# Buffers of the S5 output stage: two for the coefficients of C, the staging ring for the Toeplitz tile, results in halves

## The chip, the cores and the metric

One core of one Trainium2 chip. The metric is the device time of one execution in microseconds (us); less is better. The core has TensorE (PE; its weight loads are shown as PEld), VectorE (DVE), ScalarE (ACT), GpSimd (POOL) and SyncE (SP), which here only issues DMAs. DMAs are issued from the queues of SP and ScalarE, and 16 DMA engines carry them.

## The reference, cut to what matters

One step of a two-layer encoder over 2,192 tokens (16 meta, 2,048 of the prompt, 8 x 16 of running streams). Layer 0 is an S5 diagonal complex state-space model beside an xLSTM mLSTM; layer 1 is retention beside an RG-LRU. The change lies in the S5 part of layer 0:

```python
    _, _, h_re, h_im = lax.associative_scan(_cplx_combine, (a_re, a_im, bu_re, bu_im), axis=1)
    y = (jnp.einsum('btgp,gcp->btgc', h_re, c_re.astype(F32))
         - jnp.einsum('btgp,gcp->btgc', h_im, c_im.astype(F32)))
    y = y.reshape(bsz, T, W_A) + d.astype(F32) * uf
    y = jax.nn.gelu(y)
    y = y * jax.nn.sigmoid(y @ w_glu.astype(F32) + b_glu.astype(F32))
```

There are 32 groups of 16 channels and 64 complex states. All matrix products of the kernel that need it are made of three products of rounded halves (lines 121 to 125).

## The kernel before, in words

The kernel runs six phases; the change is in the second, `phase_l0` (line 354). This phase projects layer 0's input in three thirds of the tokens. In each third, `mtile` makes 16 tiles: 8 of the mLSTM's input (`isz` 0, with convolution and SiLU) and 8 of its gate (`isz` 1). A tile loads 512 KB of weights (line 379, on SP's queue, two buffers `wr1`), ScalarE rounds them to `wh` (line 382 by way of 105), GpSimd makes the rest `wl` (line 118), TensorE makes 48 products of 384 columns into one of four PSUM buffers (`pm1`), and ScalarE evicts them (lines 395 and 397). `values` (line 437) makes the mLSTM's values from pairs of finished tiles and needs no weights of line 379.

The normalised input of the next blocks of tokens is loaded again by `reload` (line 461): three loads per block (line 467) into the ring `ut1` of four buffers of 4 KB per partition, then `split` rounds them into `ub` (lines 105 and 109) as soon as the block that lies there has been read for the last time. There are twelve such loads.

Beside these tiles runs the generator `s5` (line 765); after each tile from the third on it is taken one step further (line 509). It has three parts:

- States (lines 772 to 859): eight steps, q = 0 to 7, of four groups each.
- Outputs (lines 861 to 936), pool `s5y`, again eight steps. For each q, `toeplitz` (line 884) loads the inputs `ur` (`s5u`, line 761), forms the coefficients `ca` (`s5ca`, lines 895 to 899) of C times the powers of the decay, multiplies them with B on TensorE (line 904), copies the result to `kp` (lines 907 and 908), writes it to HBM (line 909) and reads it back eight times, shifted, as the Toeplitz tile `tz` (`s5tz`, line 912). Then TensorE makes the outputs of two halves of 8 time steps (lines 927 to 931), ScalarE copies them to `yst` (line 934), and one DMA per half and q writes them to HBM (line 935). All tiles here have one buffer, but for the PSUM tag `s5p` with three.
- Gated unit (lines 941 to 1003), pool `s5g`: 32 loads bring the outputs back in another order (`s5gy`, line 950, on SP's queue), ScalarE takes the Gelu (line 961), and a product with `w_glu`, whose weights lie in the ring `ut1` (`p.room`, line 956), gates them. In the program this part comes in the last third (`p.loaded`, lines 485 and 938).

Program order is not the order of execution. The program is handed to a planner (`schedule_with_timeline_sim`, line 2168), which simulates it and fixes the order of the instructions on every engine and queue ahead of the run. Among instructions that are ready in its simulation the one that comes first in the program goes first; a tile takes a buffer of its tag when the first instruction that writes it is placed. On the chip each engine and queue then works strictly in that order, and an instruction that waits holds up all behind it. Pools that are closed hand their memory on tile by tile (`reuse_waits="tile"`), so the tiles of `s5g` wait for the last readers of those that lay there before.

Of the kernel before, what the change touches and what calls it, by code (L numbers as in the profile page):

```python
# [9 lines left out]
F32 = mybir.dt.float32  # L10
# [16 lines left out]
NCH = T // 16  # L27
# [10 lines left out]
def P(e, name, bufs=1, side=None):  # L38
    return e.tc.tile_pool(name=name, bufs=bufs, side=side, reuse_waits="tile")
# [6 lines left out]
def opn(e, name, bufs=1, side=None, psum=False):  # L46

    if psum:
        cm = e.tc.tile_pool(name=name, bufs=bufs, space=MemoryType.PSUM, side=side, reuse_waits="tile")
    else:  # L50
        cm = P(e, name, bufs, side)
    e.cms[name] = cm
    return cm.__enter__()
# [49 lines left out]
def split(nc, h, l, x, pool=False, act=True, fine=False):  # L103

    (nc.scalar.copy if act else nc.vector.tensor_copy)(h, x)  # L105
    if fine:
        narrow(nc, l, x, h, OP.subtract)
    else:
        (nc.gpsimd if pool else nc.vector).tensor_tensor(l, x, h, op=OP.subtract)  # L109
# [244 lines left out]
def phase_l0(e):  # L354

    nc, tc = e.nc, e.tc
# [3 lines left out]
    sb = opn(e, "b_sb", 2)  # L360
    xp = opn(e, "b_x", 2)
# [75 lines left out]
    def values(h, ut, tiles, parts):  # L437
# [8 lines left out]
        for c, nt, kind, row in tiles:  # L446
# [9 lines left out]
            nc.gpsimd.tensor_add(g, g, vo[:nt, 256:264].rearrange("p (a b) -> p a b", a=2))  # L456

    s5g = s5(e, ps)
    e.s5.loaded = False
    e.s5.room = lambda: xp.tile([128, 1024], F32R, name="ut1", bufs=4)  # L460
    def reload(bi):
        blk, b0, n = blks[bi]
        pool = e.ub_pool if bi % 3 < 2 else sb
        t = e.ub[bi] = pool.tile([128, 2, KD, 384], F32R, name=f"ub{bi % 3}", bufs=1)
        for c, nt, kind, row in blk:
            ur = xp.tile([128, KD, 128], F32, name="ut1", bufs=4)[:, :, :nt]
            nc.sync.dma_start(ur, e.u[:, :, c:c + nt])
            split(nc, t[:, 0, :, c - b0:c - b0 + nt], t[:, 1, :, c - b0:c - b0 + nt], ur)

    steps = 0  # L470
    for third in range(3):
# [6 lines left out]
        if third > 0:  # L478

            early = [mtile(third, 0, 0, ut, pg, parts),  # L480
                     mtile(third, third % 2 == 0, third % 2, ut, pg, parts)]
            for g in early:
                next(g)
            reload(2 * third + 1)
            e.s5.loaded = third == 2
# [82 lines left out]
def s5_base(e, ps):  # L568
# [4 lines left out]
    with P(e, "s5bs", side="right") as sb:  # L573
# [35 lines left out]
        v.tensor_scalar(csn, csn, -1.0, math.pi / 2, op0=OP.mult, op1=OP.add)  # L609
        nc.scalar.activation(csn, csn, AF.Sin)  # L610
        s5_phasors(v, sb, s5, csn, sn, mag, par)
        s5_turns(e, sb)

# [80 lines left out]


def s5_phasors(v, sb, s5, cs, sn, mag, par):


# [57 lines left out]
def s5_u(e, sb, q):  # L756

    ur = sb.tile([128, 2, 4, NCH], F32, name="s5u")
    gs = slice(4 * (q % 2), 4 * (q % 2) + 4)
    for hh in range(2):  # L760
        e.nc.sync.dma_start(ur[:, hh], e.ua[q // 2, 8 * hh:8 * hh + 8, :, gs, :].rearrange("s c g n -> (s c) g n"))
    return ur


def s5(e, ps):

    nc, v, tc = e.nc, e.nc.vector, e.tc
    p = e.s5
# [92 lines left out]
    with P(e, "s5y", side="right") as sb:  # L861

        pw, cc = p.pw, p.b
        for j, nm in enumerate(("re", "im")):
            cr = sb.tile([128, 4, 17, 16], F32, name="s5tm2").rearrange("p a b c -> p (a b c)")
            cr = cr[:, :512].rearrange("p (a b c) -> p a b c", a=4, b=2)
            for q in range(2):
                nc.sync.dma_start(cr[:, :, q, :], e.i["s5_c_" + nm].rearrange("a (m g) c p -> (g c) (a m) p", m=4))
            pc = ps.tile([128, 4, 128], F32, name="s5p", bufs=3)
            for m in range(4):  # L870
                nc.tensor.transpose(pc[:, m, :], cr[:, m].rearrange("p a b -> p (a b)"), e.ident)
            v.tensor_copy(cc[j].rearrange("p (m g) c -> p m (g c)", m=4), pc)


        d16 = sb.tile([128, 8], F32, name="s5d16")
        dd = sb.tile([128, 8, 16], F32, name="s5dd")
        v.memset(dd, 0.0)
        for j in range(4):
            js = slice(32 * j, 32 * j + 16)
            nc.sync.dma_start(d16[js], e.i["s5_d"].rearrange("a (q j c) -> j c (a q)", c=16, j=4)[j])  # L880
            v.tensor_tensor(dd[js], e.ident[js, None, js].to_broadcast([16, 8, 16]),
                            d16[js, :, None].to_broadcast([16, 8, 16]), op=OP.mult)

        def toeplitz(q):
            ur = s5_u(e, sb, q)
            gs = slice(4 * q, 4 * q + 4)
            cp = sb.tile([128, 2, 4, 17], F32, name="s5cp")
            v.tensor_copy(cp[UP, 0], pw[UP, 0, gs])
            v.tensor_scalar(cp[LO, 0], pw[LO, 1, gs], -1.0, None, op0=OP.mult)
            v.tensor_scalar(cp[UP, 1], pw[UP, 1, gs], -1.0, None, op0=OP.mult)  # L890
            v.tensor_scalar(cp[LO, 1], pw[LO, 0, gs], -1.0, None, op0=OP.mult)
            ca = sb.tile([128, 4, 17, 16], F32, name="s5ca")
            tmp = sb.tile([128, 4, 17, 16], F32, name="s5tm2")
            sh = [128, 4, 17, 16]
            v.tensor_tensor(ca, cp[:, 0, :, :, None].to_broadcast(sh), cc[0][:, gs, None, :].to_broadcast(sh),
                            op=OP.mult)
            v.tensor_tensor(tmp, cp[:, 1, :, :, None].to_broadcast(sh), cc[1][:, gs, None, :].to_broadcast(sh),
                            op=OP.mult)
            v.tensor_add(ca, ca, tmp)
            kp = sb.tile([128, 23, 16], F32, name="s5kp")  # L900
            v.memset(kp[:, 0:7, :], 0.0)
            pk = ps.tile([128, 256], F32, name="s5p", bufs=3)
            for j in range(4):
                nc.tensor.matmul(pk[32 * j:32 * j + 32], p.bb[:, 4 * q + j:4 * q + j + 2, :].rearrange("p a b -> p (a b)"),
                                 ca[:, j, 0:16, :].rearrange("p a b -> p (a b)"), start=True, stop=True,
                                 tile_position=(0, 32 * j), skip_group_check=True)
            nc.scalar.copy(kp[:, 7:23, :], pk.rearrange("p (a b) -> p a b", b=16))
            v.tensor_add(kp[:, 7, :], kp[:, 7, :], dd[:, q, :])
            nc.sync.dma_start(e.kp[q], kp)
            tz = sb.tile([128, 4, 16, 16], F32, name="s5tz")  # L910
            for k in range(8):
                nc.sync.dma_start(tz[16 * k:16 * (k + 1)],
                                  e.kp[q].rearrange("(g c) a b -> c g a b", g=4)[:16, :, 7 - k:23 - k, :])
            return ur, ca, tz

        for q in range(8):
            ur, ca, tz = toeplitz(q)
            for mh in range(2):
                yst = sb.tile([128, 4, NCH], F32, name="s5yst")
                for g0 in (0, 2):  # L920
                    py = ps.tile([128, 2, NCH], F32, name="s5p", bufs=3)
                    for j in range(2):
                        g = g0 + j
                        t0 = tz[:, g, 0:8, :].rearrange("p a b -> p (a b)")
                        t1 = tz[:, g, 8:16, :].rearrange("p a b -> p (a b)")
                        if mh == 0:
                            nc.tensor.matmul(py[:, j, :], t0, ur[:, 0, g, :], start=True, stop=False)
                        else:
                            nc.tensor.matmul(py[:, j, :], t1, ur[:, 0, g, :], start=True, stop=False)
                            nc.tensor.matmul(py[:, j, :], t0, ur[:, 1, g, :], start=False, stop=False)  # L930
                        nc.tensor.matmul(py[:, j, :],
                                         ca[:, g, 1 + 8 * mh:9 + 8 * mh, :].rearrange("p a b -> p (a b)"),
                                         ee[:, 4 * q + g, :], start=False, stop=True)
                    nc.scalar.copy(yst[:, g0:g0 + 2, :], py)
                nc.scalar.dma_start(e.ys[q // 2, mh, :, 4 * (q % 2):4 * (q % 2) + 4, :], yst)
            yield
    cls(e, "s5ee", "s5kb", "s5keep", "s5par")
    while not p.loaded:
# [2 lines left out]
    with P(e, "s5g", side="right") as sb:  # L941
# [47 lines left out]
        for b in range(8):  # L989
            view, n, gs = nxt  # L990
# [1108 lines left out]


PHASES = [phase_in0, phase_l0, phase_mlstm, phase_out0, phase_in1, phase_ret]


# [68 lines left out]
```

## Time and profile before

| | |
|---|---|
| Median of 3 runs (lowest, highest) | 3088.95 us (3086.74, 3089.72) |
| The profiled execution: time | 3077.24 us |
| The profiled execution: span from first to last instruction | 3075.5 us |
| Mean granted TensorE clock, as a share of full speed | 0.992 |
| Busy share of the span | TensorE 97%, VectorE 54%, ScalarE 34%, GpSimd 32% |

Times in the trace are microseconds from the start of the span. In a timeline row, the idle time of the engine ahead of the instruction stands in brackets with what ended it; a row with x3 merges three instructions in a row. "SPq" and "ACTq" are the DMA issues of SP and ScalarE.

### The profile page before, as it was taken

Reading aid. Unit: us, or ns where it says so; the run is one execution under the profiler, and the core shown is the slowest. Engines: PE = TensorE matmul, PEld = TensorE weight load, DVE = VectorE, ACT = ScalarE, POOL = GpSimd, SP = SyncE. Lnnn points to the kernel's source line nnn. Section 1 sums busy time; section 2 is a strip of 40 time slices with the busy share of each in tenths; the row PEclk is TensorE's granted clock in tenths of the full one; section 3 lists DMA queues with packets and bytes.
Section 4 is the critical chain, followed back from the end, with each engine's and each line's share of the span. In section 5 each row is a group of like instructions: output and inputs, shape, how many; then the busy total and the mean of one; then the engine's idle time right before and its main releaser. Section 6 shows DMA issues by size and latency. Waiting matters only on the chain.

```text
span 3075.5 us, 45329 instructions
## 1 busy us (share of the span) xinstructions
PE 2979.3 (97%) x17435; PEld 2696.1 (88%) x17435; DVE 1671.9 (54%) x3410; ACT 1059.5 (34%) x1860; POOL 982.1 (32%) x1160
## 2 busy tenths in 40 slices
PE   8999999998999989999999999999999999999999
PEld 7999989987988877777899999999998897888887
DVE  4845884454537772333446677767700036656563
ACT  4213443435254533211235555555511122121111
POOL 6305655445336751111111111111100024433431
PEclk9999999998999999999999999999999999999999
DMA  6447455556735557564441111111122167544442
GB/s 206 155 104 222 154 165 166 167 158 149 223 101 172 184 152 249 161 196 149 154 127 52 52 52 52 47 51 48 44 80 80 49 189 220 149 130 122 139 121 75
DMA packets 447298, 404.81 MB, mean 132 GB/s; under 512 B 43593, under 2 KB 392977, under 8 KB 447082
## 3 DMA queue, kind: packets, MB, share of 16 engines
q1 hardware_dynamic: 335340, 272.36, 31.2%
q10 hardware_dynamic: 111742, 129.56, 12.5%
q8 instruction: 137, 2.24, 0.3%
q14 instruction: 79, 0.65, 0.1%
HBM read 266.35 MB, written 135.49 MB: 131 GB/s over the span
## 4 chain that ended last, share of the span: by engine, by line
PE 61%; DVE 6%; DMA 4%; ACT 1%; issue 1%; POOL 1%; SPq 0%; DVEq 0%; POOLq 0%; ACTq 0%
PE p_pm L124 9%; PE p_pm L125 8%; PE p_pm L123 8%; PE r_pm L125 4%; PE r_pm L124 4%; PE r_pm L123 4%; PE pa L123 3%; PE pa L124 3%; PE pa L125 3%; PE pc L1388 1%; DVE p_d L1754 1%; PE pn L1385 1%; DVE p_xc L550 1%; PE r_o L1956 1%; DMA d_gb<-m_zb 1%
## 5 line engine op out<-in xcount | busy, mean ns | idle before, releaser
L123 PE MATMUL p_pm<-pu,p_wh 128*128 128x384 f32 (+1 forms) x1568 | 512.1, 327 | 0.2 <-ACT pu L105 0.2
L124 PE MATMUL p_pm<-pu,p_wh 128*128 128x384 f32 (+1 forms) x1568 | 511.8, 327 | 0.0
L125 PE MATMUL p_pm<-pu,p_wl 128*128 128x384 f32 (+1 forms) x1568 | 511.4, 326 | 0.0
L123 PE MATMUL pm<-ub,wh 128*128 128x384 f32 (+1 forms) x1136 | 377.2, 333 | 2.0 <-ACT vo L452 1.8
L124 PE MATMUL pm<-ub,wh 128*128 128x384 f32 (+1 forms) x1136 | 376.4, 331 | 1.6 <-DVE ub L109 1.6
L125 PE MATMUL pm<-ub,wl 128*128 128x384 f32 (+1 forms) x1136 | 372.9, 331 | 2.3 <-POOL wl L118 1.9
L123 PEld LDWEIGHTS p_pm<-pu,p_wh 128*128 128x128 f32 x1568 | 294.2, 188 | 1.8 <-issue 1.2
L124 PEld LDWEIGHTS p_pm<-pu,p_wh 128*128 128x128 f32 x1568 | 294.5, 188 | 1.0 <-issue 0.8
L125 PEld LDWEIGHTS p_pm<-pu,p_wl 128*128 128x128 f32 x1568 | 294.4, 188 | 0.0
L118 POOL TENSOR_TENSOR wl<-wr,wh 128x256 fp32r<-128x256 f32 x188 | 177.8, 976 | 203.7 <-ACT wh L105 203.7
L123 PEld LDWEIGHTS pm<-ub,wh 128*128 128x128 f32 x1136 | 214.4, 189 | 7.8 <-issue 4.0
L123 PE MATMUL r_pm<-roh,r_gh 128*128 128x512 f32 x544 | 218.8, 403 | 1.2 <-ACT roh L105 0.8
L125 PE MATMUL r_pm<-roh,r_gl 128*128 128x512 f32 x544 | 217.5, 401 | 1.5 <-DVE r_gl L109 1.5
L125 PEld LDWEIGHTS pm<-ub,wl 128*128 128x128 f32 x1136 | 214.4, 189 | 4.7 <-POOL wl L118 2.6
L124 PE MATMUL r_pm<-rol,r_gh 128*128 128x512 f32 x544 | 217.9, 401 | 0.4 <-DVE rol L109 0.4
L124 PEld LDWEIGHTS pm<-ub,wh 128*128 128x128 f32 x1136 | 214.7, 189 | 3.1 <-DVE ub L109 2.1
L109 POOL TENSOR_TENSOR p_wl<-p_wr,p_wh 128x1024 fp32r<-128x1024 f32 x34 | 81.8, 2406 | 385.2 <-ACT p_wh L105 385.2
L109 POOL TENSOR_TENSOR p_xcl<-p_xc,p_xch 128x384 fp32r<-128x384 f32 (+1 forms) x48 | 46.8, 976 | 245.5 <-ACT p_xch L105 209.0
L125 PEld LDWEIGHTS r_pm<-roh,r_gl 128*128 128x128 f32 x544 | 103.3, 190 | 24.0 <-DVE r_gl L109 2.4
L123 PEld LDWEIGHTS r_pm<-roh,r_gh 128*128 128x128 f32 x544 | 103.1, 190 | 22.7 <-ACT roh L105 1.3
L124 PEld LDWEIGHTS r_pm<-rol,r_gh 128*128 128x128 f32 x544 | 103.2, 190 | 21.0 <-DVE rol L109 0.7
L1754 DVE RECIPROCAL p_d<-p_d 128x384 f32<-128x384 f32 (+1 forms) x48 | 116.7, 2432 | 0.6
(731 smaller groups left out, 6751.0 us busy)
## 6 DMA issues: line engine op xcount, KB each, us to landing
wr<-in_ev_w_in_dram SPq DMA_DIRECT2D x47, 512.0 KB
p_wr<-in_od_w_in_dram SPq DMA_DIRECT2D x40, 512.0 KB
d_in<-p_o ACTq DMA_DIRECT2D x80, 192.0 KB
m_rw<-d_grow SPq DMA_DIRECT2D x18, 512.0 KB
s5u<-d_ua SPq DMA_DIRECT2D x32, 274.0 KB
d_v<-vo ACTq DMA_DIRECT2D x68, 128.0 KB
m_va<-d_v SPq DMA_DIRECT2D x17, 512.0 KB
d_h<-o_x ACTq DMA_DIRECT2D x17, 512.0 KB
```

Source lines behind the costliest of these rows:

```text
L109: (nc.gpsimd if pool else nc.vector).tensor_tensor(l, x, h, op=OP.subtract)
L118: nc.gpsimd.tensor_tensor(out[:, c], a[:, c], b[:, c], op=op)
L123: nc.tensor.matmul(out, a[0], b[0], start=start, stop=False, **kw)
L124: nc.tensor.matmul(out, a[0], b[1], start=False, stop=False, **kw)
L125: nc.tensor.matmul(out, a[1], b[0], start=False, stop=stop, **kw)
L550: v.tensor_scalar(out, x(3), pc[:, m, cw + 3:cw + 4], pc[:, m, cb:cb + 1], op0=OP.mult, op1=OP.add)
L1385: nc.tensor.matmul(pn[:n], c.qs[:, 2 * h + k, :n], ct[h][:, k, :], start=False, stop=k == 1)
L1388: nc.tensor.matmul(pc, c.kw[:n, h, 128 * k:128 * (k + 1)], c.va[:n, h, :], start=True, stop=True)
L1754: v.reciprocal(d[:, :n], d[:, :n])
L1956: nc.tensor.matmul(po, qk[:, h, :], S[:, h, :], start=False, stop=True)
```

## The change

`ca` gets two buffers. `tz` is no longer a tile of its own in pool `s5y`, but a tile of the ring `ut1`, whose four buffers serve the reloads and the weights of the gated unit as well. `yst` holds two of the four groups in place of all four, has two buffers, and is written to HBM after each copy: 32 writes of half the size in place of 16.

```diff
     e.s5.room = lambda: xp.tile([128, 1024], F32R, name="ut1", bufs=4)
+    e.s5.stage = lambda: xp.tile([128, 1024], F32, name="ut1", bufs=4)
...
-            ca = sb.tile([128, 4, 17, 16], F32, name="s5ca")
+            ca = sb.tile([128, 4, 17, 16], F32, name="s5ca", bufs=2)
...
-            tz = sb.tile([128, 4, 16, 16], F32, name="s5tz")
+            tz = p.stage().rearrange("p (g a b) -> p g a b", g=4, a=16)
...
             for mh in range(2):
-                yst = sb.tile([128, 4, NCH], F32, name="s5yst")
                 for g0 in (0, 2):
+                    yst = sb.tile([128, 2, NCH], F32, name="s5yst", bufs=2)
                     py = ps.tile([128, 2, NCH], F32, name="s5p", bufs=3)
...
-                    nc.scalar.copy(yst[:, g0:g0 + 2, :], py)
-                nc.scalar.dma_start(e.ys[q // 2, mh, :, 4 * (q % 2):4 * (q % 2) + 4, :], yst)
+                    nc.scalar.copy(yst, py)
+                    gs = slice(4 * (q % 2) + g0, 4 * (q % 2) + g0 + 2)
+                    nc.scalar.dma_start(e.ys[q // 2, mh, :, gs, :], yst)
```

## Rows read from the trace of the kernel before

**Rows 1.** The page, busy us (share of the span) and instructions of each engine.

```profile
PE 2979.3 (97%) x17435; PEld 2696.1 (88%) x17435; DVE 1671.9 (54%) x3410; ACT 1059.5 (34%) x1860; POOL 982.1 (32%) x1160
```

**Rows 2.** Busy time by stretch: stretch, length, engines, granted clock, DMA share, GB/s.

```profile
467.00:679.00 212.00, 207.33 (x1404) 198.21 (x1403) 111.08 (x160) 76.35 (x142) 99.21 (x134) 0.99 0.53 162
640.00:664.00 24.00, 20.54 (x150) 18.17 (x149) 15.91 (x34) 9.91 (x20) 10.75 (x20) 0.93 0.63 197
...
702.00:709.30 7.30, 4.32 (x26) 3.69 (x24) 3.98 (x10) 3.42 (x4) 4.01 (x8) 1.00 1.23 144
709.30:726.50 17.20, 7.00 (x33) 5.75 (x34) 4.20 (x9) 12.23 (x16) 4.79 (x9) 0.50 1.05 213
```

**Rows 3.** Timeline of TensorE, 640 to 724 us: start, length, instruction, idle before.

```profile
643.44 0.51 PE L427 MATMUL pg<-xc,gw 128*8 128x192 f32 x8 [2.49 <-ACT xc L421]
...
713.34 0.59 PE L123 MATMUL pm<-wvh,xbh 128*128 128x264 f32 x1 [5.64 <-ACT xb L397]
...
722.32 0.59 PE L123 MATMUL pm<-wvh,xbh 128*128 128x264 f32 x1 [5.03 <-ACT xb L397]
```

**Rows 4.** Timeline of ScalarE, 664 to 740 us.

```profile
697.25 1.05 ACT L105 CAST wh<-wr 128x1024 fp32r<-128x1024 f32 x1
...
710.89 2.03 ACT L961 ACTIVATE s5gy<-s5gy 128x2192 f32<-128x2192 f32 x1 [4.43 <-DMA s5gy<-d_ys]
...
718.58 1.28 ACT L961 ACT_TABLE_LOAD   x1 [2.49 <-DMA s5gy<-d_ys]
...
724.59 1.06 ACT L105 CAST wh<-wr 128x1024 fp32r<-128x1024 f32 x1
```

**Rows 5.** Timeline of SP's queue, 664 to 740 us.

```profile
671.41 0.40 SPq L379 DMA_DIRECT2D wr<-in_ev_w_in_dram  x1
679.06 31.84 SPq L950 DMA_DIRECT2D s5gy<-d_ys  x32
...
714.49 1.87 SPq L379 DMA_DIRECT2D wr<-in_ev_w_in_dram  x2
```

**Rows 6.** Timelines of TensorE, SP and VectorE, 526 to 551 us: one round.

```profile
526.85 0.40 PE L931 MATMUL s5p<-s5ee,s5ca 128*128 128x137 f32 x2
527.05 0.82 SPq L761 DMA_DIRECT2D s5u<-d_ua  x2
527.53 1.72 DVE L895 TENSOR_TENSOR s5ca<-s5cp,s5b 128x1088 f32<-128x1088 f32 x1
...
535.45 0.32 SPq L909 DMA_DIRECT2D d_kp<-s5kp  x1
538.26 3.61 SPq L912 DMA_DIRECT2D s5tz<-d_kp  x8
...
545.33 0.39 PE L927 MATMUL s5p<-s5u,s5tz 128*128 128x137 f32 x2
...
550.46 0.40 PE L931 MATMUL s5p<-s5ee,s5ca 128*128 128x137 f32 x2
```

**Rows 7.** Timeline of TensorE, 676 to 679 us: the loop's last matmuls.

```profile
678.63 0.40 PE L931 MATMUL s5p<-s5ee,s5ca 128*128 128x137 f32 x2
```

**Rows 8.** Instructions on the ring `ut1`: least, median, most ns, first and last start.

```profile
L467 SPq DMA_DIRECT2D ut<-d_u x12: 518/914/3193, 252.4 to 419.0; - x12
L105 ACT CAST ub<-ut x12: 1038/1048/1052, 260.8 to 604.7; 128x1024 fp32r<-128x1024 f32 x12
```

**Rows 9.** Waits of VectorE, ScalarE and TensorE, 467 to 727 us: total, times, longest.

```profile
DVE s5ca L895 <- PE s5p L931: 16.4, 4, 13.9
...
ACT s5yst L934 <- DMA d_ys<-s5yst: 11.7, 5, 2.6
...
PE s5p L927 <- DMA s5tz<-d_kp: 1.2, 1, 1.2
```

**Rows 10.** The writes of the results, ScalarE's queue: least, median, most ns.

```profile
L935 ACTq DMA_DIRECT2D d_ys<-s5yst x16: 326/327/477, 497.7 to 682.7; - x16
```

## The prediction

> **What bounds the kernel now.** I read the page's busy shares first. TensorE is busy 97% of the span [rows 1]; so a change that takes no matmul away can only win back the few stretches in which TensorE stands still or runs at its lower clock. Next I read the busy time by stretch, to find which of those the edited code can reach [rows 2]. The edited loop over q runs from 467 to 679 us, and there TensorE is busy 207.33 of 212 us: little is lost beside it. The loss comes right behind it: from 702 to 726.5 us TensorE is busy 4.32 of 7.30 us and 7.00 of 17.20 us, and in the second stretch the granted clock is 0.50, the 1.2 GHz level. That is 2.98 + 10.20 = 13.2 us idle, and 7.00 us of work at half clock, which would take 3.5 us at full clock: 16.7 us in all. A smaller loss lies at 640 to 664 us: 24 - 20.54 = 3.5 us idle, and a clock of 0.93, that is 0.07 x 24 = 1.7 us; 5.2 us in all.
>
> Then the waits. TensorE's two long ones, 5.64 and 5.03 us, end with ScalarE's eviction at line 397 [rows 3]. ScalarE was not busy: its queue stood at the Gelu of line 961, which waited 4.43 and 2.49 us for the `s5gy` loads [rows 4]. Those are 32 loads that hold the SP queue for 31.84 us without a break, from 679.06 on [rows 5]; the DMA engines are full meanwhile (share 1.23 and 1.05) [rows 2]. Two weight loads of line 379 stand behind them in that queue: the one before was issued at 671.41, the next two at 714.49 and after [rows 5]. So TensorE ran out of weights as well: the conversion of the next weights (line 105, `wh`) comes at 724.59, where the last one was at 697.25 [rows 4]. The loads cannot start earlier, since they need the memory of the S5 loop: they begin with its last matmul, at 679 [rows 7]. The S5 loop is a chain that trails behind, and its end sets where this burst falls.
>
> **The change part by part.** One round of the chain [rows 6]: the last matmul of a q ends at 527.25; DVE begins `ca` of the next q at 527.53; `kp` is written at 535.45, read back as `tz` from 538.26 with eight issues (3.61 us); the matmuls begin at 545.33 and end at 550.86. That is 23.6 us; over the six rounds from 527.25 to 679.0 the mean is 25.3 [rows 6, 7].
>
> *Two buffers for `ca`.* The stretch from `ca` to the landed `kp`, 538.26 - 527.25 = 11.0 us, can now run beside the matmuls of the q before. The DVE waits for `ca` go (16.4 us, four times) [rows 9]; DVE is not the bound, so they count only through the chain.
>
> *`tz` in the staging ring.* The ring has four buffers, and the reloads take them first: all twelve loads are issued by 419.0, but the last are converted only at 604.7 [rows 8]. So the three of the last block hold three buffers, and one is left for `tz` until then. `tz` is thus no better buffered than before for most of the loop; its loads wait for the last matmul that reads the old one. `ur` keeps its one buffer too. What stays in the round: 0.82 (`ur` issues) + 3.61 (`tz` issues) + at most 545.33 - 541.87 = 3.5 (landing and TensorE's queue) + 5.5 (the matmuls) = 13.4 us [rows 6]. The first q ends near 502 as before, so the loop ends near 502 + 7 x 13.4 = 596 us, some 80 us earlier. That frees no engine: it moves the burst.
>
> *Results in halves.* 16 issues more on ScalarE's queue at 327 ns [rows 10] are 5.2 us, in 212 us of which ScalarE is busy 76 [rows 2]: nothing while it waits for others that long; 5.2 us if they all came ahead of an eviction. In return the wait for the single buffer goes (11.7 us over five waits [rows 9]), again beside TensorE. I count zero for both.
>
> *The burst, moved.* It now falls into the second third of the tiles. There the weight loads come before the `s5gy` loads in program order, so the planner lets a weight load pass as soon as its buffer is free, where now the waiting loads belong to tiles behind the burst. I take a weight load to be held for half the burst, 16 us, in place of nearly the whole. A load is normally issued 697.25 - 671.41 = 25.8 us ahead of its conversion, and the late one shows that 724.59 - 714.49 = 10.1 us do [rows 4, 5]: 15.7 us of slack. So the weights would come just about in time. I leave 5 us of the 16.7 us, for Gelus that still block ScalarE a few us each, and count 11.7 us won; the bounds are 0 and 16.7.
>
> *The loss at 640 to 664.* It is one wait of 2.49 us for the convolution [rows 3] and what follows. DVE's waits for `ca` push such convolutions back, but other waits do so too. Half, 2.6 us; bounds 0 and 5.2.
>
> *New waits of TensorE.* With 13 us in place of 25 between two q's, `tz` comes with less to spare. Before, one wait of 1.2 us shows it [rows 9]. I take two: 2.4 us lost. The bounds are nothing, and 3.5 us (the landing above) at each of seven q's, 24.5 us.
>
> The sum is -11.7 - 2.6 + 2.4 = -11.9 us, against the profiled execution: 3077.2 us become 3065. That execution stood 11.7 us under the median of the runs, 3088.95; I carry the difference over to the median: 3077.
>
> **The rivals.**
> *The stall only moves.* The 32 loads are as many as before, and fill the DMA engines wherever they fall; if the planner again puts them in one block, with a weight load behind them, the 13.2 us of idle time come back 80 us earlier and nothing is won: 3089, or 3086 with the 2.6 us. For it: in rows 5 the planner has placed all 32 without a break. Against it: the order of the program now favours the weights. The Trainium skill (Perfetto Trace Analysis, "Identifying the Most-Contended Engine") has a rule that would give this result: a kernel improves by improving its most-contended engine, which here is TensorE, and the change takes nothing off it; by that the time stays at 3089. The trace agrees with the rule up to 702 us and not in the 25 us behind.
>
> *The chain hardly shortens.* `kp`, `cp`, the scratch tile and `ur` keep one buffer each, and the change would do little of what it says. With a round of 20 us the loop ends near 642, and the burst falls on the last third, as now: about 3086.
>
> *Everything is won.* No weight load is late, and no wait is new: 16.7 + 5.2 = 21.9 us, 3067.
>
> *Slower: TensorE waits in place for `tz`.* Its order is fixed before the run. If the planner takes the loads to be faster than they are, each q's matmuls stand at the head of TensorE's queue before `tz` is there, and all tiles behind them wait. At the bound of 3.5 us that is 24.5 us for seven q's, and a clock that falls after each can add 1.7 us each, as at 640 to 664: some 36 us at most, 30 in the middle. Against the 14.3 us won: 3089 + 30 - 14 = 3105. It decides from 2 us per q. For it: the wait of 1.2 us [rows 9] came with a chain of 25 us. Against it: that was one in eight.
>
> **How the numbers follow.** A measurement of this kernel can tell about 0.2%, 6.2 us, from no change; so faster is below 3082.8 and slower above 3095.1. Chances: the forecast 0.43, of which 0.38 is beyond 0.2%; everything won 0.15; the stall only moves 0.20 (0.04 faster, 0.13 same, 0.03 slower); the chain hardly shortens 0.10 (0.03, 0.06, 0.01); TensorE waits for `tz` 0.12. That sums to 0.60 faster, 0.24 same, 0.16 slower. The range reaches from just below "everything is won", 3064, to 3095; above it lies most of the slower rival and part of those around no change; the forecast's own range is 3070 to 3084.
>
> **What would show it.** Right: the last matmul of line 931 near 600 in place of 679, rounds near 13 us; `tz` loads issued right behind the matmuls of the q before; the 32 `s5gy` loads begin near 600, with loads of line 379 among them; no stretch of 17 us at half clock behind them. Wrong: a stretch with TensorE idle over 10 us and a gap of 30 us between weight loads where the burst now is (the stall moved); rounds of 20 us and more (the chain); waits of line 927 for `s5tz` of 2 us or more at most q's (slower). A time under 3060 would mean that I have missed a loss that hangs on the S5 loop; one over 3110, that the reloads wait for the ring, which I have excluded because they are loaded before `tz` asks for it [rows 8].

## The result, and the profile after

The changed kernel takes 3160.05 us (median of four runs, 3156.8 to 3165.93) against 3088.12 us of the kernel before beside it: a ratio of 1.0238, with an interval of 1.0223 to 1.0252. It is 72 us slower, where 12 us of gain were forecast; the time lies above the range and above the forecast's slower rival as well. The profiled execution took 3156.8 us, with a span of 3155.0; that is 79.6 us above the profiled execution of the kernel before, which lay below its own median.

In the kernel after, line numbers are one or two higher: the reloads' loads are L468, the `tz` loads L913 (their tile now shows as `ut`, the ring), the matmuls of `pk` L905, the last matmuls of a q L932, the result loads L952. The page's busy row first; it answers to [rows 1]:

```profile
PE 2987.4 (95%) x17435; PEld 2705.3 (86%) x17435; DVE 1662.5 (53%) x3410; ACT 1062.4 (34%) x1862; POOL 974.8 (31%) x1160
```

The matmuls are as many, and their busy time hardly rose (2979.3 to 2987.4 us); what grew is the time in which TensorE does nothing. The busy time by stretch tells where, first for the kernel after (stretch, length, PE, PEld, DVE, ACT, POOL, granted clock, DMA share, GB/s):

```profile
425.00:800.00 375.00, 278.99 (x1767) 264.98 (x1768) 153.22 (x232) 125.21 (x213) 142.29 (x201) 0.85 0.54 139
428.00:440.00 12.00, 1.98 (x7) 1.14 (x7) 8.70 (x28) 0.00 (x0) 0.00 (x0) 0.50 0.20 37
440.00:535.00 95.00, 37.85 (x241) 34.29 (x242) 33.96 (x59) 12.07 (x27) 0.00 (x0) 0.65 0.40 113
535.00:600.00 65.00, 64.96 (x451) 61.70 (x449) 30.34 (x37) 25.04 (x47) 30.86 (x38) 1.00 0.72 213
600.00:632.00 32.00, 21.31 (x115) 20.27 (x114) 5.65 (x6) 12.82 (x16) 13.48 (x19) 0.85 1.17 162
632.00:660.00 28.00, 15.85 (x80) 14.84 (x81) 0.00 (x0) 15.09 (x21) 8.91 (x21) 0.68 0.85 159
```

And the same long stretch of the kernel before:

```profile
425.00:800.00 375.00, 348.83 (x2360) 332.24 (x2359) 196.09 (x294) 153.25 (x290) 186.74 (x281) 0.97 0.56 154
```

From 425 to 800 us TensorE is busy 278.99 us where it was 348.83: 69.84 us less, the larger part of the 79.6 us between the two profiled executions. The largest piece is 440 to 535 us: 95 - 37.85 = 57.2 us idle, at a clock of 0.65, with GpSimd doing nothing at all. A second one, 22.8 us idle, lies at 600 to 660, and is told of below.

What was TensorE waiting for? Waits in the stretch 380 to 560 us of the kernel after (who waits, for whom: total, times, longest):

```profile
POOL wl L118 <- ACT wh L105: 131.0, 5, 117.4
...
DVE s5ca L896 <- PE s5p L932: 53.0, 5, 11.9
PE s5p L928 <- DMA ut<-d_kp: 50.3, 5, 10.4
```

By TensorE's row alone this would be the forecast's slower rival: TensorE waits for `tz`, five times about 10 us. But GpSimd's row says more: the split of the next weights stood still for 117.4 us. Work for the tiles of the blocks had stopped altogether. TensorE waits for `tz` because nothing else is there to be done, as its timeline shows (start, length, instruction, idle before):

```profile
464.82 0.40 PE L932 MATMUL s5p<-s5ee,s5ca 128*128 128x137 f32 x2
465.15 0.64 PE L905 MATMUL s5p<-s5ca,s5bb 128*32 128x256 f32 x8
475.85 0.80 PE L928 MATMUL s5p<-s5u,ut 128*128 128x137 f32 x2 [10.06 <-DMA ut<-d_kp]
```

The bare chain of S5 runs here, q after q, with no tile's matmul between. Who stopped the tiles is read from SP's queue:

```profile
414.31 0.49 SPq L379 DMA_DIRECT2D wr<-in_ev_w_in_dram  x1
...
453.10 3.61 SPq L913 DMA_DIRECT2D ut<-d_kp  x8
...
521.88 3.60 SPq L913 DMA_DIRECT2D ut<-d_kp  x8
525.52 2.54 SPq L468 DMA_DIRECT2D ut<-d_u  x3
...
541.02 3.60 SPq L913 DMA_DIRECT2D ut<-d_kp  x8
545.58 6.38 SPq L379 DMA_DIRECT2D wr<-in_ev_w_in_dram  x2
...
578.77 4.13 SPq L913 DMA_DIRECT2D ut<-d_kp  x8
582.95 2.65 SPq L468 DMA_DIRECT2D ut<-d_u  x3
...
597.88 10.01 SPq L952 DMA_DIRECT2D s5gy<-d_ys  x8
608.00 0.39 SPq L379 DMA_DIRECT2D wr<-in_ev_w_in_dram  x1
608.44 19.31 SPq L952 DMA_DIRECT2D s5gy<-d_ys  x18
```

Only three reload loads (block 2) are issued early, by 255 us; [rows 8] had all twelve out by 419.0. The next three (block 3, which the second third needs) come at 525.52, right behind the `tz` loads of the fifth q, and the last six behind those of the eighth. Between 414.31 and 545.58 no weight load of line 379 is issued. In the text of the program `reload(3)` stands behind five rounds of the S5 loop and ahead of the other three. So **the buffers of the ring were given out in the order of the program**: block 3 had to wait until five `tz` tiles, which come before it in the text, had had theirs, and each of those hangs on the chain of S5.

A free buffer was not lacking. VectorE reads the last tile of block 2 here (line 109), and is done with it at 268.8 us:

```profile
267.14 1.66 DVE L109 TENSOR_TENSOR ub<-ut,ub 128x1024 fp32r<-128x1024 f32 x1
```

From then to the first `tz` at 453.10 nothing is loaded into the ring's four buffers, and block 3 is not loaded either.

### The profile page after: what moved, and what is told of

The parts are those of the page before. It is cut to its first block, busy times and chain, and to the rows that moved or that the text cites. A ratio compares the mean times of both kernels' runs of the same rounds, so it can differ in the third digit from the quotient of the medians.

```text
span 3155.0 us, 45356 instructions
## 1 busy us (share of the span) xinstructions
PE 2987.4 (95%) x17435; PEld 2705.3 (86%) x17435; DVE 1662.5 (53%) x3410; ACT 1062.4 (34%) x1862; POOL 974.8 (31%) x1160
## 4 chain that ended last, share of the span: by engine, by line
PE 74%; DVE 12%; DMA 8%; issue 2%; ACT 2%; POOL 1%; SPq 1%; ACTq 1%; DVEq 0%; POOLq 0%
PE p_pm L124 8%; PE p_pm L125 8%; PE p_pm L123 8%; PE pm L125 4%; PE pm L123 4%; PE pm L124 4%; PE r_pm L125 4%; PE r_pm L124 4%; PE r_pm L123 4%; PE pa L123 3%; PE pa L124 3%; PE pa L125 3%; DVE p_d L1756 1%; PE pc L1390 1%; DMA m_rw<-d_grow 1%
## 5 line engine op out<-in xcount | busy, mean ns | idle before, releaser
L118 POOL TENSOR_TENSOR wl<-wr,wh 128x256 fp32r<-128x256 f32 x188 | 171.1, 941 | 280.9 <-ACT wh L105 280.9
```

Source lines behind the costliest of these rows:

```text
L118: nc.gpsimd.tensor_tensor(out[:, c], a[:, c], b[:, c], op=op)
```

## The experiments

The theory from these rows: the loss is the shared ring given out in program order; nothing else in the change costs much. Rivals: the two `ca` buffers or the halves cost it; or TensorE's order simply puts it in front of a late `tz`. Two `ca` buffers beside an own `tz` tile were not run; the ring with one `ca` buffer was, twice.

**The ring alone.** The kernel before, with `tz` from the ring and nothing else of the change:

```
-            tz = sb.tile([128, 4, 16, 16], F32, name="s5tz")
+            tz = p.stage().rearrange("p (g a b) -> p g a b", g=4, a=16)
```

> The kernel before with one edit: the Toeplitz tile lies in the staging ring; the coefficients of C keep one buffer and the results are written whole. Theory A (the ring is given out in program order, so the three loads of the block that the second third needs wait until five Toeplitz tiles have had their buffers): slower by at least 60 us, 3150 to 3200 us, with the loads of line 467 issued behind the fifth Toeplitz load and TensorE idle in between. Theory B (the second buffer of the coefficients lets the planner pull the S5 loop together, so that TensorE waits for each Toeplitz tile): within 10 us of 3088. Theory C (TensorE waits in place because the halves and the denser loop delay the loads): within 10 us of 3088 as well.

3166.09 us, a ratio of 1.0264 (1.0228 to 1.0301). Waits of its TensorE:

```profile
PE s5p L928 <- DMA ut<-d_kp: 44.1, 5, 9.2
...
PE s5p L905 <- DVE s5ca L900: 14.6, 5, 3.4
```

And SP's queue where block 3 comes:

```profile
531.31 3.60 SPq L913 DMA_DIRECT2D ut<-d_kp  x8
534.96 2.37 SPq L468 DMA_DIRECT2D ut<-d_u  x3
```

Block 3 again follows the fifth `tz`. The ring by itself brings the whole loss. The second row is a wait that the second `ca` buffer takes away but for 3.4 us (once, in the kernel after).

**The halves alone.** The kernel before, with the results stored in halves:

```
-                yst = sb.tile([128, 4, NCH], F32, name="s5yst")
                 for g0 in (0, 2):
+                    yst = sb.tile([128, 2, NCH], F32, name="s5yst", bufs=2)
...
-                    nc.scalar.copy(yst[:, g0:g0 + 2, :], py)
-                nc.scalar.dma_start(e.ys[q // 2, mh, :, 4 * (q % 2):4 * (q % 2) + 4, :], yst)
+                    nc.scalar.copy(yst, py)
+                    gs = slice(4 * (q % 2) + g0, 4 * (q % 2) + g0 + 2)
+                    nc.scalar.dma_start(e.ys[q // 2, mh, :, gs, :], yst)
```

> The kernel before with one edit: the results in halves with two buffers. Theories A and B: within 6 us of 3088, since ScalarE's waits for the single buffer lay beside TensorE's work. Theory C: slower by 20 us or more.

3086.83 us, a ratio of 1.0008 (0.9994 to 1.0022): no difference.

**The reloads ahead of `tz` in the text.** If the order of the program is what matters, moving one call should undo the loss, with all three parts of the change in place. First block 3 alone:

```
                 if m == 4:
                     reload(2 * third + 2)
+                    if third == 0:
+                        reload(3)
...
-            reload(2 * third + 1)
+            if third == 2:
+                reload(2 * third + 1)
```

> The changed kernel with the reload of block 3 called in the first third, right behind that of block 2, so that its three tiles come ahead of the Toeplitz tiles in the ring. Theory A: the stall from 428 to 535 us goes, at least 60 of the 72 us come back, 3080 to 3105 us. Theories B and C: the Toeplitz waits of TensorE at line 928 stay near 10 us each and the time over 3140 us.

3083.09 us against 3083.54 before, a ratio of 0.9993 (0.9979 to 1.0007). The 72 us are gone, and six reload loads now go out by 269 us:

```profile
250.44 7.82 SPq L468 DMA_DIRECT2D ut<-d_u  x4
...
269.34 0.52 SPq L468 DMA_DIRECT2D ut<-d_u  x1
```

TensorE's waits for `tz`, 50.3 us over five in the kernel after, are 10.5 over two here, with one of 8.9 left. Next, block 4 as well, at the start of the second third, ahead of the last three `tz`:

```
                 if m == 4 and third == 0:
                     reload(2)
                     reload(3)
...
-            reload(2 * third + 1)
+            reload(4 if third == 1 else 5)
```

> As the run before, and the reload of block 4 called at the start of the second third as well, ahead of the last three Toeplitz tiles; that of block 5 stays. Theory A: as the run before or up to 15 us faster, 3070 to 3100 us, since no reload stands behind Toeplitz tiles that are later than it. Theories B and C: over 3140 us.

3077.45 us, a ratio of 0.9978 (0.9962 to 0.9993): faster than the kernel before, by 6 us. The same order of reloads in the kernel before, as a control:

> The kernel before with nothing changed but the order of the reloads (block 3 loaded in the first third, block 4 at the start of the second). Theory (the order matters only where the ring is shared; what made the due-order run 0.22% faster is the change itself): no change, within 0.1% of before, 3081 to 3088. Rival (the reload order alone gives the gain, by moving loads out of the crowded end of the second third): 3074 to 3080.

3086.88 us, a ratio of 1.0000 (0.9989 to 1.0010). So the order alone shows no gain; what is 0.22% faster is the change, once the ring is asked in the right order. Where so small a gain lies is hard to read from single executions, which differ by more than that; two stretches say something on it. First the control:

```profile
400.00:430.00 30.00, 26.32 (x172) 25.23 (x171) 24.63 (x28) 16.01 (x31) 15.62 (x18) 0.94 0.73 220
425.00:800.00 375.00, 346.47 (x2327) 329.66 (x2326) 191.46 (x286) 151.07 (x286) 186.36 (x280) 0.96 0.55 150
```

Then the changed kernel in due order:

```profile
400.00:430.00 30.00, 30.00 (x207) 29.10 (x207) 22.72 (x28) 15.77 (x35) 15.75 (x21) 1.00 0.45 141
425.00:800.00 375.00, 349.56 (x2354) 333.15 (x2354) 204.70 (x301) 157.00 (x293) 182.03 (x278) 0.96 0.61 165
664.00:692.00 28.00, 18.30 (x110) 16.57 (x111) 10.49 (x15) 17.46 (x25) 14.20 (x26) 0.76 0.93 207
```

Some of the gain seems to lie before the S5 loop, at 400 to 430 us (DMA share 0.45 against 0.73). The four profiled kernels with `tz` in its own tile are idle 1.9 to 3.7 us there, and the five in due order 0.04 us at most. The loads of the later blocks, five of them there in the kernel before, are held back by the ring to 567 us and after in this run. That these loads cause the idle time is argued, not shown: TensorE's waits there end with ScalarE's copies at line 452. The last row is the stall behind the burst, and it is still there, at 664 to 692 instead of 702 to 726: 9.7 us idle, and a clock of 0.76.

**Does a shorter loop pay?** In the run in due order a round takes (636.8 - 497.1) / 7 = 20.0 us, not the 13.4 of the forecast. Its `ca` was ready one q ahead, but `pk` came right behind the last matmul of the q before, at 497.36 behind one that began at 497.03:

```profile
497.03 0.40 PE L933 MATMUL s5p<-s5ee,s5ca 128*128 128x137 f32 x2
497.36 0.64 PE L906 MATMUL s5p<-s5ca,s5bb 128*32 128x256 f32 x8
```

`pk` shares the PSUM tag `s5p`, with three buffers, with the four output tiles of a q, which stand before it in the text: the same rule in another memory. So `pk` got a tag of its own, and `s5p` one buffer less:

```
-            pk = ps.tile([128, 256], F32, name="s5p", bufs=3)
+            pk = ps.tile([128, 256], F32, name="s5k", bufs=1)
```

> Theory (PSUM buffers of a tag are given out in program order, so that pk of q+1 waits for q's four output tiles though its coefficients are ready): with pk in a tag of its own, pk of q+1 starts before the last S5 matmul of q, the rounds fall from 17 to 21 us to 13 to 15, and the loop ends at 580 to 600 in place of 637. The burst of result loads moves with it, to about 600 to 632, and the hole behind it with it, so that the time changes little: 3070 to 3080. Rival (the rounds are set by the ring buffer of tz or by the chain from ca to kp itself): rounds stay at 17 to 21 us, loop end near 637, 3077.

3076.66 us, a ratio of 0.9978 (0.9968 to 0.9987). TensorE's timeline of that kernel:

```profile
472.50 0.64 PE L906 MATMUL s5k<-s5ca,s5bb 128*32 128x256 f32 x8
478.67 0.64 PE L906 MATMUL s5k<-s5ca,s5bb 128*32 128x256 f32 x8
489.47 0.47 PE L929 MATMUL s5p<-s5u,ut 128*128 128x137 f32 x2 [1.19 <-DMA d_kp<-s5kp]
...
497.13 0.40 PE L933 MATMUL s5p<-s5ee,s5ca 128*128 128x137 f32 x2
```

`pk` of the second q (478.67) is done before the first q's matmuls begin. The rounds fall to (603.1 - 497.2) / 7 = 15.1 us, and the loop ends at 603 in place of 637. The time is the same. SP's queue says why:

```profile
603.96 32.72 SPq L953 DMA_DIRECT2D s5gy<-d_ys  x32
638.95 0.39 SPq L958 DMA_DIRECT2D s5zt<-in_s_w_glu_dram  x1
639.81 4.00 SPq L379 DMA_DIRECT2D wr<-in_ev_w_in_dram  x2
```

The stretch behind the burst, in the columns of the stretches above:

```profile
630.00:665.00 35.00, 24.76 (x124) 23.43 (x125) 4.64 (x6) 20.91 (x32) 14.23 (x30) 0.74 0.87 182
```

The burst starts where the loop ends, weights stand behind all 32 loads again, and 10.2 us are idle behind it. The stall has moved with the loop, as one rival had it.

The other direction, one `ca` buffer in due order:

```
-            ca = sb.tile([128, 4, 17, 16], F32, name="s5ca", bufs=2)
+            ca = sb.tile([128, 4, 17, 16], F32, name="s5ca")
```

> The reloads in due order with the ring tile and the halves, but one ca buffer. Theory (a shorter loop doesn't shorten the kernel, since the hole behind the burst of result loads moves with the loop's end): the rounds go back to 22 to 27 us, the loop ends at 670 to 700, and the time is within 0.15% of the 3077 with two buffers, 3073 to 3082. Rival (as the forecast had it, that a faster loop pays): 5 to 12 us slower than with two buffers, 3082 to 3090.

3098.33 us, a ratio of 1.0028 (1.0015 to 1.0042): by the two ratios 0.5% slower than with two, and beyond both expectations. The rounds take 23.4 us, and the loop ends at 659. The stretch ahead of its end, in that kernel:

```profile
624.00:659.30 35.30, 15.18 (x97) 14.13 (x97) 9.19 (x14) 6.38 (x12) 0.00 (x0) 0.66 0.49 142
```

TensorE is idle 20.1 us there. SP's queue gives the reason:

```profile
646.38 3.60 SPq L914 DMA_DIRECT2D ut<-d_kp  x8
650.02 2.26 SPq L468 DMA_DIRECT2D ut<-d_u  x3
```

The last three reload loads come behind the last `tz`, at 650.02, and the tiles at hand had run out at 624. With two buffers the same loads go out at 628.70, in time. So in a shared ring the end of the loop does count, but only as the time by which the next tiles can be loaded; once they are in time, ending it 34 us earlier wins nothing. My theory of that run, that the loop's length does not matter, was too simple.

**The stall behind the burst.** The 32 result loads read pieces of 137 floats, 548 bytes. Laid out so that a row of 8.8 KB is read, they become four loads; the writes become 64 stores in place of 16 (or of 32 with halves):

```
-    e.ys = dram.tile([4, 2, 128, 8, NCH], F32, name="d_ys")
+    e.ys = dram.tile([4, 8, 16, 2, 8, NCH], F32, name="d_ys")
...
-                nc.scalar.dma_start(e.ys[q // 2, mh, :, 4 * (q % 2):4 * (q % 2) + 4, :], yst)
+                for j in range(4):
+                    nc.scalar.dma_start(e.ys[q // 2, 4 * (q % 2) + j, :, mh].rearrange("c t n -> t c n"), yst[:, j, :])
...
-            for g in range(8):
-                src = e.ys[mt].rearrange("h (t c) g n -> c g (h t) n", c=16)
-                nc.sync.dma_start(gy[mt][16 * g:16 * g + 16], src[:, g])
+            nc.sync.dma_start(gy[mt], e.ys[mt].rearrange("g c h t n -> (g c) (h t) n"))
```

On the kernel before:

> The kernel before with the S5 results laid out in memory so that they come back in 4 loads with rows of 8.8 KB in place of 32 loads in pieces of 548 bytes (and are written in 64 stores in place of 16). Theory (the hole of 16.7 us behind the loop is the weight load queued behind the short pieces, which take 31.8 us): the loads take some 12 to 20 us, the weight loads behind them land in time, the hole shrinks to 0 to 6 us, and the time is 3072 to 3080. Rival (the amount of bytes sets it, not the pieces, or the hole has another cause): loads still take 30 us, the hole stays, 3085 to 3092.

3076.35 us, a ratio of 0.9976 (0.9965 to 0.9988). Its SP queue, which answers to [rows 5]:

```profile
676.07 13.54 SPq L379 DMA_DIRECT2D wr<-in_ev_w_in_dram  x2
689.70 5.33 SPq L949 DMA_DIRECT2D s5gy<-d_ys  x4
...
708.35 10.88 SPq L379 DMA_DIRECT2D wr<-in_ev_w_in_dram  x2
```

And three stretches of it:

```profile
425.00:800.00 375.00, 356.37 (x2403) 339.30 (x2402) 202.42 (x297) 150.87 (x291) 189.60 (x282) 0.98 0.52 157
...
700.00:711.00 11.00, 11.00 (x69) 11.00 (x68) 5.43 (x8) 11.00 (x16) 7.79 (x13) 1.00 0.92 355
...
709.30:726.50 17.20, 14.21 (x84) 13.19 (x83) 14.45 (x22) 12.41 (x21) 17.13 (x27) 0.80 0.52 162
```

The loads hold the queue for 5.33 us in place of 31.84, and TensorE is busy 356.37 us of the long stretch in place of 348.83: 7.5 us more. The two medians are 8.3 us apart, and the two profiled executions 4.8. Behind the loop, from 702 to 726.5 us, 3.0 us are idle in place of 13.2 [rows 2]. The planner also put two weight loads right ahead of these loads, so shorter transfers and a better place in the queue are not told apart here.

With long rows in the changed kernel in due order:

> The changed kernel with reloads in due order and the long rows. Theory: the hole of 14.5 us behind the burst shrinks to 0 to 6 us, 3062 to 3070. Rival (bytes, not pieces): no change against the 3077 of the run without the long rows, 3075 to 3080.

3081.65 us, a ratio of 0.9987 (0.9978 to 0.9997): a miss; it is no faster than without. One wait of its TensorE stands out:

```profile
PE s5p L929 <- DMA ut<-d_kp: 12.2, 3, 10.2
```

10.2 us of it come at the last q (matmuls from 640.01 us); the loads of block 5, behind it in the ring, go out at 637.94, 9 us later than in the run without long rows. That looks like the stall of the one `ca` buffer again. Why the chain came later was not settled. Nor do the four loads hold SP's queue as briefly as in the kernel before with long rows: 14.64 us in place of 5.33, while they wait for the writes of the results (line 951, for `d_ys<-s5yst`: 18.6 us over three waits). With long rows and `pk` in its own tag:

> The changed kernel with reloads in due order, pk in a PSUM tag of its own and the long rows. Theory: loop end at 580 to 600 and no hole behind it: 3058 to 3070. Rival (bytes, not pieces; or the end of the loop doesn't matter): as the run with pk in its own tag alone, 3070 to 3080.

3075.58 us, a ratio of 0.9969 (0.9958 to 0.9981): the best of all, and below both kernels, though its interval overlaps that of the long rows alone and that of `pk` in its own tag alone. As a forecast it missed, and the rival's range holds it: the loop ended at 619, the four loads held the queue for 14.40 us, and from 615 to 665 us TensorE is still idle 5.4 us.

## Why the prediction was wrong

**The step that failed** is "*`tz` in the staging ring*": "The ring has four buffers, and the reloads take them first". I read [rows 8] as the order in which buffers are taken, and thought that a tile takes its buffer when its first writer is placed, as I had also written of the kernel before. The reloads were early there only because nothing else asked for the ring. The runs showed the order of the program in its place: block 3 behind five `tz` tiles in both kernels with the ring, and no loss as soon as the text asked for block 3 first. It cost 72 us. My last sentence had named the case ("the reloads wait for the ring") and excluded it by that reading; the call of `reload(3)` in the text, behind five rounds of S5, would have answered it.

The other steps are best held against the run in due order, where this one is mended.

- *Two buffers for `ca`*: `ca` came one q ahead, as forecast, but the round came to 20.0 us in place of 13.4, since `pk` waited for PSUM; with that mended, 15.1. That `pk` shares a tag with the output tiles was in the code, and I had missed it. DVE's waits for `ca` did not go, as I had said they would; 16.4 us over four before, they are more in the run in due order, now for the matmuls two q's back:

```profile
DVE s5ca L897 <- PE s5p L933: 37.0, 5, 15.1
```

- *Results in halves*: zero, as forecast (1.0008).
- *The burst, moved*: wrong. I had counted 11.7 of 16.7 us as won. In the changed kernel the weight loads did come among the burst, in groups of 8, 18 and 6, and TensorE still stood idle 22.8 us at 600 to 660. ScalarE's queue stood at the Gelu there, 22.0 us over four waits (line 963), where I had left 5 us of TensorE's time for it. In due order all 32 stood in one block again, and 9.7 us were idle behind it; so they did with `pk` in its own tag, where the loop ended at 603, near the 596 of the forecast, and 10.2 us were idle. The rival "the stall only moves" was right on this.
- *The loss at 640 to 664*: not won. TensorE's waits for the convolution (line 427) are 8.4 us over four in due order, from 400 to 900 us, and 3.6 over two in the kernel before.
- *New waits of TensorE*: 2.4 us forecast; 3.3 us over two waits in due order. The 50.3 us in the kernel after come from missing other work: with the reloads ahead they fell to 10.5 and 3.3 us, while `tz` still came by the same chain.
- *The slower rival* gave the right sign with the wrong mechanism; its bound of 36 us took 3.5 us of wait per q, where the five waits of the kernel after took 9.57 to 10.38, with no other work in TensorE's queue.

With the mend the change is worth 6 us, and the burst, where I had looked for the gain, did not give it. That the run in due order lands on 3077 us, the figure of the forecast, is chance: the kernel before took 3083.54 beside it, and two of the three terms came out otherwise.

The Trainium skill (Perfetto Trace Analysis, "Optimization Strategy") says that the same gap repeated on the engine that should be full can mean too few buffers for the next tile. The trace agrees as to the sign, five gaps of 9.57 to 10.38 us, but not as to the cure: the ring kept its four buffers, and moving one call left two waits, 10.5 us together, and moving two 3.3 us.

## What to carry to other kernels

Before a tile moves into a shared ring, write down who asks for the ring, in the order of the program's text, and when each gives its buffer back; a slow chain in front of an early load makes the load as late as the chain. Where an engine waits again and again for a small chain, look at what the other engines do in that time: if they do nothing, the question is who stopped the other work. In these runs the burst at the end of the loop moved with the loop, and shortening the loop paid only where something waited for its end.

## What was not expected of the hardware

The 32 result loads in pieces of 548 bytes (137 KB each) hold the DMA engines full at a low rate: 144 GB/s at a share of 1.23 from 700 to 711 us in the kernel before. With rows of 8.8 KB the same stretch shows 355 GB/s at 0.92, and ScalarE and TensorE busy throughout. The Trainium skill (DMA: Bandwidth & Descriptors, "Specifications") gives 512 bytes as the least transfer for full rate; 548 bytes were far from it here, by these two rows, though the stretches hold other transfers too.
